# Relative-bias Toeplitz tile: read from one copy of the row and turned round on GpSimd, in place of a 128-fold copy in DRAM

## The chip, the cores and the metric

The kernel runs on one core of one Trainium2 chip. The metric is the device time of one execution in microseconds; before the change it is 1153.88 us, the median of three runs (1153.59 to 1154.02).

## The reference

One decoder layer over 256 tokens of width 2048, all in float32. After a first RMS norm one input projection gives the queries, keys and values of two groups of eight heads (head size 128) and eight forget logits. The first group ("fox") attends causally, with a bias that is a difference of cumulated log forget gates. The second group ("dilated") attends in three patterns of dilation 1, 4 and 16, mixed by their softmax denominators; its bias depends only on the head and on the distance of query and key. Each group's output is normed, both are projected and added to the residual, and a squared-ReLU MLP (2048 to 8192 to 2048) and a final RMS norm follow.

```
logits = einsum('bdhnqe,bdhnke->bdhnqk', qb, kc) * scale
bias   = rel_bias[rel_bucket(clip(rel, 0, span) * dilation)]     # by distance only
logits = logits + bias[None, None, :, None]
```

## The kernel before

**Main stream.** Every weight matrix is read in chunks of 512 columns, and a chunk in steps of 256 rows (two 128-row tiles, `j` = 0 and 1). For each step ScalarE rounds the raw weights to `whi` (L168) and VectorE writes the remainder `wlo` = raw - whi (L169); TensorE then multiplies three terms (L299 to L301, or L313 where the result is wanted turned). For the input projection a step is 12 matmuls. Steps are counted in slots, two to a step; at slot `2*i + j` the side work that was registered with `at(slot, ...)` is emitted right behind the products of that half step. All engines run their own instructions in the order in which they are emitted.

**Supply.** Before the products of step `i`, the splits up to step `i + LEAD` are emitted (`LEAD` = 3), and with the split of step `k` the DMA for step `k + LEAD + 2`, on the SyncE queue; a DMA carries two steps (1 MB) into one of four buffers `raw`. `whi` and `wlo` have four buffers each.

**Around the change.** The first three chunks are q, v and k of four fox heads. The forget logits come with the v chunk, whose last slot is 31. Four slots later `rel_tiles` is emitted: TensorE multiplies the table `relx` with the constant `pick` into a row of 384 biases for each of eight heads (L414), VectorE copies it to SBUF (L416, 8 partitions), and two DMAs on the GpSimd queue follow. L418 writes the row 128 times to DRAM (`rel_d`, 8 x 128 x 384); L419 reads it back with a pitch of 383 per partition, so that partition p gets the row moved by p: that is `relT` (128 x 8 x 256). L419 needs what L418 wrote.

**What is behind it on GpSimd.** `decay_of` (L465) makes the forget-gate operand `gate_h` of a head from `gate_t`; it has two buffers, is emitted three slots before that head's scores, and the first matmul of the scores reads it (L482). The first four heads' scores are at slots 53, 57, 61 and 65, their `values` eleven slots later; each `values` but the first adds a square on GpSimd (L538). The next four fox heads have their scores from slot 101. `relT` is first read by the scores of the third group of heads (L495), whose k chunk is the ninth. Much later `relT` takes the final gains (`load_gf`, L592).

**Buffers.** `big_lo` (`yT_lo`) has 16 head slots; the last eight (`yT_lo[:, NH:, :]`) are first written by `values` of the dilated heads.

Of the kernel before, what the change touches and what calls it, by code (L numbers as in the profile page):

```python
# [11 lines left out]
F32 = mybir.dt.float32  # L12
# [7 lines left out]
P = 128  # L20
D_MODEL = 2048
SEQ = 256
TB = SEQ // P
HD = 128
NH = 8
# [10 lines left out]
RW = 3 * P  # L36
# [6 lines left out]
def _constants():  # L43
    i = np.arange(P)
    upto = (i[:, None] <= i[None, :]).astype(np.float32)
    after = (i[:, None] > i[None, :]).astype(np.float32)
    tri = np.where(i[None, :] <= i[:, None], 0.0, NEG).astype(np.float32)
    head = (i[:, None] % 32 == np.arange(NH)[None, :]).astype(np.float32)
    pack = np.concatenate([after, -upto, tri, np.zeros((P, P), np.float32), tri, head], axis=1)

    dist = 255 - np.arange(RW)
    d = np.maximum(dist, 0)
    exact = N_BUCKETS // 2
    df = np.maximum(d.astype(np.float32), np.float32(1.0))
    large = exact + (
        np.log(df / np.float32(exact)) / np.float32(math.log(REL_MAX / exact)) * np.float32(N_BUCKETS - exact)
    ).astype(np.int32)
    bucket = np.where(d < exact, d, np.minimum(large, N_BUCKETS - 1))
    count = np.zeros(RW, np.int64)
    for window, dil in PATTERNS:  # L60
        count += (dist >= 0) & (dist % dil == 0) & (dist <= window)
    pick = np.zeros((N_BUCKETS + 1, RW), np.float32)
    pick[bucket, np.arange(RW)] = 1.0
    pick[N_BUCKETS] = np.where(count > 0, np.log(np.maximum(count, 1)), NEG)
    return np.ascontiguousarray(pack), pick
# [3 lines left out]
def kernel(  # L69
# [18 lines left out]
    nc = tc.nc  # L88
# [9 lines left out]
    dram = ctx.enter_context(tc.tile_pool(name="dram", bufs=1, space=DRAM))  # L98
# [240 lines left out]
    def at(i, f, *a):  # L339
        side.setdefault(i, []).append((f, a))  # L340
# [66 lines left out]

    relT = one.tile([P, NH, SEQ], F32, name="relT")  # L410

    def rel_tiles():
        p = psum.tile([P, 512], F32, name="sc")
        nc.tensor.matmul(p[:NH, :RW], relx, pick_sb, start=True, stop=True)  # L414
        row = two.tile([P, RW], F32, name="neg")[:NH]
        nc.vector.tensor_copy(row, p[:NH, :RW])  # L416
        d = dram.tile([NH, P, RW], F32, name="rel_d")
        nc.gpsimd.dma_start(d, row[:, None, :].to_broadcast([NH, P, RW]))  # L418
        nc.gpsimd.dma_start(  # L419
            relT, bass.AP(tensor=d.tensor, offset=d.offset + P - 1, ap=[[RW - 1, P], [P * RW, NH], [1, SEQ]])  # L420
        )


    qkv = {}
    yT_hi = one.tile([P, 2 * NH, SEQ], F32R, name="big_hi")
    yT_lo = one.tile([P, 2 * NH, SEQ], F32R, name="big_lo")
# [240 lines left out]
    for ci, (what, key, *_rest) in enumerate(chunks[:-1]):  # L667
        e = last_slot[what, key]
        if what == "v":
            at(e, drain_v, key, ci)  # L670
            if key == 0:
                at(e, drain_f)
                at(e + 2, forget_gates)
                at(e + 6, gate_sums)
                at(e + 4, rel_tiles)
        elif what in "qk":
            late = 3 if ci == 0 else 0
            at(e + late, drain_qk, key, what, ci)
            at(e + late + 2, turn_qk, key, what, 0)
            at(e + late + 3, turn_qk, key, what, 1)  # L680
            if what == "k":
                kind = groups[key][4]
                for h in range(4):
                    n = e + 6 + 4 * h
                    if kind == 0:
                        at(n - 3, decay_of, groups[key][3] * 4 + h)
                    at(n, scores, key, h)
                    at(n + 6, turn_probs, key, h)
                    at(n + 11, values, key, h)
                    if h == 3 and key % 2:  # L690
                        at(n + 13, group_norm, kind)
        elif what == "o":
            at(e, drain_o, *key, ci)
            if key[0] == 1:
                at(e + 2, to_features, 4 * key[1], 16)
                at(e + 3, to_features, 4 * key[1] + 2, 16)
                if key[1] == 3:
                    at(e + 4, second_norm)
        elif what == "u":
            at(e, drain_u, key[1], ci)  # L700
        else:
            at(e, drain_d, *key, ci)
            if key == (ROUNDS - 1, 0):
                at(e - 8, load_gf)
# [68 lines left out]
```

## Time and profile before

| what | value |
|---|---|
| median of 3 runs | 1153.88 us |
| profiled execution | 1154.59 us |
| its span on the core | 1152.8 us |
| mean granted TensorE clock | 0.989 |
| TensorE matmul busy | 1126.7 us, 98% |
| VectorE / ScalarE / GpSimd busy | 55% / 45% / 3% |

The profiled execution's time is 1.8 us longer than the span of the trace, which lies between its first and last instruction. The page says for each engine how long it was busy; the chain of work that ended last goes back from the last instruction, at each step to what released it. A granted clock of 1.00 is 2.4 GHz, 0.50 is 1.2 GHz.

### The profile page before, as it was taken

To read this page: it belongs to the slowest core of one execution; us is meant where nothing else is said; L and a number is where in the kernel's file an instruction comes from. 1 tells how busy PE (TensorE), PEld (TensorE's weight loads), DVE (VectorE), ACT (ScalarE), POOL (GpSimd) and SP (SyncE) were. 2 spreads that over 40 slices of the span, in tenths; PEclk is the share of its full clock that TensorE was granted. 3 is DMA by queue.
4 is the path that set the end of the run, shared out by engine and by line. 5 is a ranking of instruction groups with operands and counts; after the bars stand their busy time and mean duration, and the time that the engine had idled before them with its cause. 6 is when DMAs were issued, how large, how long until landed. Compare 5 with 4: busy or idle time off the path is not lost.

```text
span 1152.8 us, 16038 instructions
## 1 busy us (share of the span) xinstructions
PE 1126.7 (98%) x6635; PEld 991.0 (86%) x6635; DVE 638.9 (55%) x795; ACT 522.0 (45%) x675; POOL 29.4 (3%) x56
## 2 busy tenths in 40 slices
PE   9994999999999999999999999999999999999997
PEld 6773888888888889998889998889999889999886
DVE  5652655656647665555454555544555554555564
ACT  5442544544545455444433544333444343444441
POOL 0100000000000100000000000000000000000000
PEclk9997999999999999999999999999999999999999
DMA  9666455454454455655566465566546666555641
GB/s 314 213 159 161 139 181 183 146 182 147 157 192 162 159 173 180 198 199 189 184 197 195 156 217 184 190 201 194 183 159 209 198 201 183 183 183 184 248 153 73
DMA packets 105605, 210.71 MB, mean 183 GB/s; under 512 B 3987, under 2 KB 4836, under 8 KB 105404
## 3 DMA queue, kind: packets, MB, share of 16 engines
q1 hardware_dynamic: 104556, 207.06, 55.0%
q0 software_dynamic: 976, 2.63, 1.5%
q8 instruction: 52, 0.85, 0.3%
q14 instruction: 21, 0.17, 0.0%
HBM read 206.00 MB, written 3.67 MB: 182 GB/s over the span
## 4 chain that ended last, share of the span: by engine, by line
PE 95%; issue 3%; DVE 1%; DMA 0%; POOL 0%; ACT 0%; SPq 0%; DVEq 0%; POOLq 0%; ACTq 0%
PE acc L313 31%; PE acc L299 20%; PE acc L300 20%; PE acc L301 20%; PE sc L485 1%; PE sc L530 1%; PE tr L250 1%; PE tr L455 1%; PE tr L512 0%; DMA grow<-in_norm_g_dram 0%; PE sc L333 0%; PE sc L482 0%; POOL rel_d L418 0%; ACT L380 0%; DVE wlo L169 0%
## 5 line engine op out<-in xcount | busy, mean ns | idle before, releaser
L169 DVE TENSOR_TENSOR wlo<-raw,whi 128x1024 fp32r<-128x1024 f32 (+1 forms) x381 | 463.3, 1222 | 376.8 <-ACT whi L168 374.0
L168 ACT ACTIVATE whi<-raw 128x1024 fp32r<-128x1024 f32 (+1 forms) x381 | 399.9, 1055 | 406.7 <-PE acc L300 242.9
L313 PE MATMUL acc<-aT_hi,whi 128*128 128x256 f32 x1024 | 287.3, 281 | 0.0
L313 PE MATMUL acc<-aT_lo,whi 128*128 128x256 f32 x1024 | 286.1, 279 | 0.0
L313 PE MATMUL acc<-aT_hi,wlo 128*128 128x256 f32 x1024 | 286.1, 279 | 0.0
L299 PE MATMUL acc<-whi,big_hi 128*128 128x512 f32 (+1 forms) x632 | 246.0, 389 | 0.0
L301 PE MATMUL acc<-wlo,big_hi 128*128 128x512 f32 (+1 forms) x632 | 244.7, 387 | 0.0
L300 PE MATMUL acc<-whi,big_lo 128*128 128x512 f32 (+1 forms) x632 | 244.6, 387 | 0.0
L313 PEld LDWEIGHTS acc<-aT_hi,wlo 128*128 128x128 f32 x1024 | 192.9, 188 | 0.0
L313 PEld LDWEIGHTS acc<-aT_hi,whi 128*128 128x128 f32 x1024 | 192.3, 188 | 0.2
L313 PEld LDWEIGHTS acc<-aT_lo,whi 128*128 128x128 f32 x1024 | 191.7, 187 | 0.2
L299 PE MATMUL acc<-whi,aT_hi 128*128 128x512 f32 x384 | 157.9, 411 | 0.0
L300 PE MATMUL acc<-whi,aT_lo 128*128 128x512 f32 x384 | 153.4, 400 | 0.0
L301 PE MATMUL acc<-wlo,aT_hi 128*128 128x512 f32 x384 | 153.0, 398 | 0.0
L301 PEld LDWEIGHTS acc<-wlo,big_hi 128*128 128x128 f32 x632 | 118.7, 188 | 24.5
L300 PEld LDWEIGHTS acc<-whi,big_lo 128*128 128x128 f32 x632 | 118.8, 188 | 23.2
L299 PEld LDWEIGHTS acc<-whi,big_hi 128*128 128x128 f32 x632 | 118.8, 188 | 23.1
L301 PEld LDWEIGHTS acc<-wlo,aT_hi 128*128 128x128 f32 x384 | 73.1, 190 | 17.6
L299 PEld LDWEIGHTS acc<-whi,aT_hi 128*128 128x128 f32 x384 | 73.3, 191 | 15.4 <-issue 0.6
L300 PEld LDWEIGHTS acc<-whi,aT_lo 128*128 128x128 f32 x384 | 73.4, 191 | 14.2 <-DVE aT_lo L240 0.3
L499 ACT ACTIVATE pr<-neg,st 128x128 f32<-128x128 f32 (+1 forms) x32 | 14.3, 448 | 56.2 <-DVE st L495 56.2
L237 DVE TENSOR_TENSOR big_lo<-nat,big_hi 128x512 fp32r<-128x512 f32 x32 | 22.2, 693 | 22.4 <-ACT big_hi L236 22.4
(159 smaller groups left out, 532.9 us busy)
## 6 DMA issues: line engine op xcount, KB each, us to landing
raw<-in_w_mlp_in_dram SPq DMA_DIRECT2D x64, 1024.0 KB, 5.3
raw<-in_w_mlp_out_dram SPq DMA_DIRECT2D x64, 1024.0 KB, 5.3
raw<-in_w_in_dram SPq DMA_DIRECT2D x42, 1024.0 KB, 5.2
raw<-in_w_out_dram SPq DMA_DIRECT2D x16, 1024.0 KB, 5.1
raw<-in_w_in_dram SPq DMA_DIRECT2D x4, 1040.0 KB, 5.3
raw<-in_w_in_dram SPq DMA_DIRECT2D x3, 512.0 KB, 7.5
xs<-in_x_dram SPq DMA_DIRECT2D x3, 512.0 KB, 9.0
rel_d<-neg POOLq DMA_DIRECT2D x1, 1536.0 KB, 36.6
```

The lines of the kernel that those rows point to most:

```text
L168: nc.scalar.activation(hi, t, AF.Copy)
L169: nc.vector.tensor_tensor(lo, t, hi.bitcast(F32), op=ALU.subtract)
L237: nc.vector.tensor_tensor(lo, src, hi.bitcast(F32), op=ALU.subtract)
L250: nc.tensor.transpose(p[:, j * SEQ + t * P:j * SEQ + (t + 1) * P], xs[:, t, c:c + P], ident)
L299: nc.tensor.matmul(acc, xh, hi[:, j, cols], start=go, stop=False)
L300: nc.tensor.matmul(acc, xl, hi[:, j, cols], start=False, stop=False)
L301: nc.tensor.matmul(acc, xh, lo[:, j, cols], start=False, stop=end)
L313: nc.tensor.matmul(acc, w[:, j, b * P:(b + 1) * P], a[:, kt, :], start=kt == 0 and b % 2 == 0 and n == 0, stop=kt == kts - 1 and n == 2, s ...
L455: nc.tensor.transpose(p[:, j * SEQ + t * P:j * SEQ + (t + 1) * P], ts[t][:, h * P:(h + 1) * P], ident)
L485: nc.tensor.matmul(s[:, c0:c1], q[:, h, t * P:(t + 1) * P], k[:, h, :c1 - c0], start=n == 0 and kind == 1, stop=n == 2,)
L499: nc.scalar.activation(pr[:, c0:c1], neg[:, c0:c1], AF.Exp, bias=st[:, 0, t:t + 1], scale=-1.0, accum_out=st[:, 1, t:t + 1],)
L530: nc.tensor.matmul(y[:, o0:SEQ], v[:, t, h * P:(h + 1) * P], p[:, c0:c1], start=t == 0 and n == 0, stop=t == 1 and n == 2,)
```

## The change

The constant `pick` is built with distances rising instead of falling (`np.arange(RW) - 127`), so the row of biases runs the other way. The row is written to DRAM once (8 x 384). A second DMA reads it with a pitch of 1 per partition, 8 x 256 elements into the unused half of `big_lo`; the keys there run from last to first. A copy on GpSimd with a step of -1 writes `relT` in the right order. The three parts are emitted at slots 35, 36 and 86 (`e` is 31); the second waits for the first, the third for the second.

```
-    dist = 255 - np.arange(RW)
+    dist = np.arange(RW) - 127
...
     relT = one.tile([P, NH, SEQ], F32, name="relT")
-
-    def rel_tiles():
+    rel_d = dram.tile([NH, RW], F32, name="rel_d")
+
+    def rel_row():
         p = psum.tile([P, 512], F32, name="sc")
         nc.tensor.matmul(p[:NH, :RW], relx, pick_sb, start=True, stop=True)
         row = two.tile([P, RW], F32, name="neg")[:NH]
         nc.vector.tensor_copy(row, p[:NH, :RW])
-        d = dram.tile([NH, P, RW], F32, name="rel_d")
-        nc.gpsimd.dma_start(d, row[:, None, :].to_broadcast([NH, P, RW]))
+        nc.gpsimd.dma_start(rel_d, row)
+
+    def rel_back():
         nc.gpsimd.dma_start(
-            relT, bass.AP(tensor=d.tensor, offset=d.offset + P - 1, ap=[[RW - 1, P], [P * RW, NH], [1, SEQ]])
+            yT_lo[:, NH:, :].bitcast(F32), bass.AP(tensor=rel_d.tensor, offset=rel_d.offset, ap=[[1, P], [RW, NH], [1, SEQ]])
         )
+
+    def rel_turn():
+        back = yT_lo[:, NH:, :].bitcast(F32)
+        nc.gpsimd.tensor_copy(relT, bass.AP(tensor=back.tensor, offset=back.offset + SEQ - 1,
+                                            ap=[back.ap[0], back.ap[1], [-1, SEQ]]))
...
-                at(e + 4, rel_tiles)
+                at(e + 4, rel_row)
+                at(e + 5, rel_back)
+                at(e + 55, rel_turn)
```

## Rows read from the trace of the kernel before

**Rows 1.** The page: TensorE's busy time, and its granted clock in 40 slices.
```profile
PE 1126.7 (98%) x6635; PEld 991.0 (86%) x6635; DVE 638.9 (55%) x795; ACT 522.0 (45%) x675; POOL 29.4 (3%) x56
...
PEclk9997999999999999999999999999999999999999
```

**Rows 2.** Chain that ended last, in time: start us, length us, what.
```profile
72.22 1.32 POOL rel_d L418
73.54 35.55 issue
109.13 0.90 POOL relT L419
110.07 0.50 POOL gate_h L465
```

**Rows 3.** Waits of PE: us in total, times, longest us.
```profile
PE sc L482 <- POOL gate_h L465: 15.0, 1, 15.0
```

**Rows 4.** Timeline of PE: start us, us, line, operation, out<-in.
```profile
91.68 0.39 PE L301 MATMUL acc<-wlo,aT_hi 128*128 128x512 f32 x1
...
95.18 0.40 PE L301 MATMUL acc<-wlo,aT_hi 128*128 128x512 f32 x1
110.62 0.47 PE L482 MATMUL sc<-gate_h,gate_s 128*128 128x128 f32 x1 [15.04 <-POOL gate_h L465]
...
112.49 0.63 PE L299 MATMUL acc<-whi,aT_hi 128*128 128x512 f32 x1
...
117.17 0.39 PE L301 MATMUL acc<-wlo,aT_hi 128*128 128x512 f32 x1
...
120.20 0.22 PE L482 MATMUL sc<-gate_h,gate_s 128*128 128x128 f32 x1
...
121.11 0.39 PE L299 MATMUL acc<-whi,aT_hi 128*128 128x512 f32 x1
```

**Rows 5.** Windows: from:to, length, PE's granted clock, DMA share, GB/s.
```profile
95.00:100.00 5.00, 1.00 0.49 64
100.00:105.00 5.00, 0.51 0.51 68
```

**Rows 6.** DMA issues: out<-in, queue, times, KB each, median us to landing.
```profile
rel_d<-neg POOLq DMA_DIRECT2D x1, 1536.0 KB, 36.6
relT<-rel_d POOLq DMA_DIRECT2D x1, 1024.0 KB, 8.8
relT<-in_final_norm_g_dram SPq DMA_DIRECT2D x1, 1024.0 KB, 7.4
out_dram<-xs SPq DMA_DIRECT2D x4, 256.0 KB, 2.4
...
relx<-in_rel_bias_dram SPq DMA_DIRECT2D x1, 1.0 KB, 7.8
```

**Rows 7.** Timeline of POOL.
```profile
49.11 0.20 POOL L158 CAST wf<-raw 128x16 fp32r<-128x16 f32 x1 [3.22 <-PE sc L333]
...
155.15 0.73 POOL L538 TENSOR_TENSOR sq<-sq,sqt 128x256 f32<-128x256 f32 x1 [5.53 <-ACT sqt L536]
155.87 0.93 POOL L465 TENSOR_SCALAR gate_h<-gate_t,pk 128x256 fp32r<-128x256 f32 x2
...
376.00 1.59 POOL L538 TENSOR_TENSOR sq<-sq,sqt 128x256 f32<-128x256 f32 x1 [5.75 <-ACT sqt L536]
```

**Rows 8.** Timeline of DVE.
```profile
90.20 0.69 DVE L237 TENSOR_TENSOR k_lo<-tr,k_hi 128x512 fp32r<-128x512 f32 x1 [1.68 <-ACT k_hi L236]
...
375.76 1.22 DVE L169 TENSOR_TENSOR wlo<-raw,whi 128x1024 fp32r<-128x1024 f32 x1
```

**Rows 9.** Windows of L169 on DVE, then of L301 on PE and PEld: busy (instructions).
```profile
0.00:95.41 95.41, 36.11 (x31) 0.98 0.72 221
...
0.00:95.41 95.41, 43.00 (x108) 20.60 (x108) 0.98 0.72 221
```

**Rows 10.** Tile raw from 40 to 140 us: landing times of its loads.
```profile
DMA to landing us min/median/max: 4.9/5.6/32.2
```

## Prediction

> **What bounds the kernel now.** I read the page first: TensorE's matmuls are busy 98% of the span, and the granted clock is low in one slice only after the start, the fourth, 86 to 115 us [rows 1]. So TensorE is the bound, and a change elsewhere counts only through a hole in its stream. The view of waits, for TensorE alone, has one long row: 15.0 us, once, for `gate_h` of L465 [rows 3]. The chain of waits says where that comes from [rows 2]: L418 issues the 128-fold copy at 72.22 us; the next 35.55 us no engine does anything that the chain can name; then L419, and only behind it `gate_h` at 110.07. GpSimd works in order, L419 waits for what L418 wrote, and L465, which needs nothing of either, stands behind L419. That the wait is the copy's is in the DMA view: the 1536 KB of `rel_d` take 36.6 us from issue to landing [rows 6].
>
> **What the wait costs.** The last product before the hole starts at 95.18 us; the row 15 matmuls earlier starts at 91.68, so the pitch is 0.233 us and the scores were due at 95.41. They start at 110.62: 15.21 us lost [rows 4]. A second loss follows. The clock is 1.00 from 95 to 100 us and 0.51 from 100 to 105, that is, it falls from 2.4 to 1.2 GHz inside the idle time [rows 5], and TensorE starts again slow. From 110.62 to 117.17 it runs 19 matmuls, the eight of the scores and eleven products, in 6.55 us. At the full clock the same eight scores take 0.91 us (120.20 to 121.11) and eleven products 11 x 0.233 = 2.56: 3.47 us. Lost: 3.08 us [rows 4]. Together 18.29 us.
>
> **The change part by part.** *The constant and the matmul:* the same sizes; zero by construction.
>
> *L418, now 12 KB instead of 1536 KB, and the wait of `rel_back` for it.* No row shows a 12 KB write on this queue. From below: 2.4 us, the stores of 256 KB to DRAM. From above: the old 36.6 us, if the time were fixed and not that of the bytes; against that speaks the other DMA of the same queue, which lands 1024 KB in 8.8 us, so there is no fixed cost above 8.8 [rows 6]. A load of 1 KB between weight loads took 7.8 us. I take 5 us, nearer to the small transfers; ends 2.4 and 8.8. Issue as before 1.32 us, so `rel_back` goes out at 72.22 + 1.32 + 5 = 78.5 us (75.9 to 82.3), takes 0.90 us on GpSimd as L419 does, and the two waiting `gate_h` another 0.93 [rows 2, 7]: done at 80.4 us (77.8 to 84.2), where the scores want them at 95.41. Eleven microseconds are to spare at the late end. The hole is gone if the 12 KB land in under 95.41 - 73.54 - 1.83 = 20 us.
>
> *`rel_back`:* the same 1 MB in the same pieces of 1 KB as L419, which landed in 8.8 us; what is new is that all partitions read the same 12 KB. The load of the final gains also reads one 8 KB row for all 128 partitions, and lands 1024 KB in 7.4 us [rows 6]. I take 8.8; bounds 7.4 and 36.6 (if it fared like `rel_d`). Nothing on GpSimd waits for it before `rel_turn`. In exchange the 36.6 us write leaves the DMA engines: beside it one weight load took 32.2 us where the median is 5.6 [rows 10]. TensorE showed no wait for that, because it was standing still; so no gain is booked, but the weights are better off, not worse.
>
> *`rel_turn`, 128 x 2048 on GpSimd.* It is emitted at slot 86, behind the third square sum of the first heads (slot 76), whose row is at 155.15 us and would move to 136.9. GpSimd is idle there until the `gate_h` of the next heads, which have run at 155.87 until now and are wanted for slot 101. That is 15 slots of half a step (6 x 0.233 = 1.4 us) behind slot 86, 21 us at least. Its length is on no row. Two sizes of one-input work are: 0.20 us for 16 elements per partition and 0.47 for 256 (half of 0.93), so 0.27 / 240 = 1.1 ns an element and 0.20 + 2032 x 0.0011 = 2.5 us. From above by a plausible row, eight times the two-input sum of 0.73: 5.8 us; from above by any row, 16 elements in 0.20 us, 12.5 ns each: 25.6 us [rows 7]. I take 3 us, near the one-input rows; a step of -1 has no row and is why the upper end is kept.
>
> It can cost something only through VectorE. A square sum that starts at 376.00, while `wlo` runs from 375.76 to 376.98, lasts until 377.59, 0.61 after that end, against 0.73 alone [rows 7, 8]: GpSimd did nothing until `wlo` was over. No row shows the opposite, a `wlo` kept waiting by GpSimd. If it waits as long as the copy runs, `wlo` is up to 3 us late. Cover: at 95.41 TensorE had done 108 matmuls of L301, four to a step, so 27 steps; VectorE had begun 31 `wlo`, of which the first two are halves of one step, so 30 steps [rows 9]. The newest `wlo` is thus wanted two whole steps later, 2 x 12 x 0.233 = 5.6 us, some 6 with its own rest. A turn of up to 6 us costs nothing, one of T us costs about T - 6; with 3 us zero, by the bounds 0 to 19.6 us.
>
> The Trainium skill, "SBUF — State Buffer", section "Who interferes with whom", says that a VectorE instruction with two SBUF inputs and a GpSimd instruction that reads SBUF exclude each other, for the whole of whichever starts first. The trace agrees where VectorE was first, 1.59 us against 0.73; no run here shows the other order. By that rule a `wlo` would wait out the whole copy; by the row alone it need not wait; with 6 us of cover the sum is the same, and the rule is the rival below when the copy is long. The skill's "GPSIMD Engine Reference", section 3.1, gives 1.8 cycles an element at best for one-input loops, which would make 3.1 us at 1.2 GHz, an estimate from that page.
>
> *What is late next,* at the scores of slot 53: `k_lo` of those heads is written at 90.89 [rows 8], before 95.41, and three split steps are in hand [rows 9]. The other sets of scores wait for nothing, by the same view in which the 15.0 is the one long row [rows 3].
>
> **Sum.** 1154.59 (profiled) - 15.21 - 3.08 + 0 = 1136.3 us. The profiled execution is 0.71 above the median of the runs, so the median goes from 1153.88 to 1135.6.
>
> **Rivals.** (a) *The turn blocks VectorE for longer than its cover.* With T between 6 and 15 us TensorE waits 0 to 9 us around 140 us, without the clock loss while the hole is under the 4 us or so that it took to fall [rows 5], with 3.1 us beyond: 1135.6 to 1147.7; I give 1139 at T = 9.4. For it: the excluding seen at 376 us. Against: the one-input rows at 1.1 ns.
> (b) *The read of one hot row is slow and starves the weights.* If `rel_back` takes 36.6 us and holds a weight load for 32.2 [rows 10], that load, issued five steps (14.0 us) ahead of its split and 6 more ahead of its use, is 12 us late; with 3.1 of clock 1150.7. Against: the gains' load at 7.4 us.
> (c) *The wait is not one of bytes* and `rel_back` still holds GpSimd for 36 us: the hole stays, 1154. Against: 8.8 us on the same queue.
> (d) *Slower:* `rel_turn` costs what the tiny casts cost, 12.5 ns an element, 25.6 us. Then `wlo` stops for that time at about 138 us, TensorE for 25.6 - 6 = 19.6 and 3.1 us of slow clock on top: 22.7 - 18.3 = 4.4 slower, 1158.3. It decides from T = 6 + 18.3 - 3.1 = 21.2 us on, 10.3 ns an element. For it: only that a backward step is on no row.
>
> **Chances.** Forecast 0.82 with its own spread of 1134 to 1137.5; (a) 0.09; (b) 0.03; (c) 0.03; (d) 0.03. The range 1133.5 to 1141 takes in the forecast and most of (a). About 0.2% (2.3 us) is what a measurement of this kernel can tell from no change. Faster is the forecast, (a) and (b), 0.94; same is (c), 0.03; slower is (d), 0.03.
>
> **What would show it.** Right: no wait of TensorE for `gate_h`; the two `gate_h` at about 80 us; granted clock 1.00 from 95 to 120 us; products following the first scores at a pitch of 0.233; a `rel_turn` of 2.5 to 6 us at about 137 us with at most one `wlo` pushed back and no hole in TensorE behind it; no weight load over 10 us between 72 and 90. Wrong: `rel_back` issued after 93 us, a wait of TensorE for `wlo` around 140 us, or a `rel_turn` beyond 6 us.

## The result and the profile after

The changed kernel takes 1137.01 us (median of 4, 1136.27 to 1137.23) against 1153.74 us before: a ratio of 0.9855 with a 95% interval of 0.9838 to 0.9872, 16.7 us. The forecast was 1135.6 us, the range 1133.5 to 1141. The profiled execution took 1136.86 us, 17.73 less than that of before; its span is 1135.1 us.

GpSimd after the change (timeline: start us, length us, line, operation, out<-in):

```profile
72.81 0.76 POOL L419 DMA_DIRECT2D rel_d<-neg  x1 [22.62 <-DVE neg L418]
77.00 0.96 POOL L422 DMA_DIRECT2D big_lo<-rel_d  x1 [3.44 <-DVE wlo L169]
78.00 0.94 POOL L473 TENSOR_SCALAR gate_h<-gate_t,pk 128x256 fp32r<-128x256 f32 x2
...
137.47 0.73 POOL L546 TENSOR_TENSOR sq<-sq,sqt 128x256 f32<-128x256 f32 x1 [5.53 <-ACT sqt L544]
138.15 1.90 POOL L428 COPY relT<-big_lo 128x2048 f32<-128x2048 f32 x1
140.03 1.90 POOL L473 TENSOR_SCALAR gate_h<-gate_t,pk 128x256 fp32r<-128x256 f32 x2
```

The read-back goes out 4.2 us after the write, where it took 36.9 before [rows 2], and the two `gate_h` are ready at 78.9 us, 17 us before they are wanted. (The view names `wlo` as what released the read-back; in a second profile of the change it names the 12 KB write itself, 3.66 us of idle time, and the write landed there in 4.1.) The issues, KB and us to landing:

```profile
big_lo<-rel_d POOLq DMA_DIRECT2D x1, 1024.0 KB, 7.3
...
rel_d<-neg POOLq DMA_DIRECT2D x1, 12.0 KB, 3.9
```

TensorE, its waits (us in total, times, longest) and its stream at the first scores:

```profile
PE sc L220 <- DVE relx L199: 1.2, 1, 1.2
PE tr L250 <- DVE aT_lo L240: 0.8, 1, 0.8
PE tr L227 <- DMA grow<-in_norm_g_dram: 0.5, 1, 0.5
```

```profile
95.76 0.40 PE L301 MATMUL acc<-wlo,aT_hi 128*128 128x512 f32 x1
95.99 0.22 PE L490 MATMUL sc<-gate_h,gate_s 128*128 128x128 f32 x1
...
96.91 0.39 PE L299 MATMUL acc<-whi,aT_hi 128*128 128x512 f32 x1
...
102.51 0.22 PE L490 MATMUL sc<-gate_h,gate_s 128*128 128x128 f32 x1
```

The 15.0 us row for `gate_h` [rows 3] is gone; what is left are three waits of the start. The scores follow the products at the pitch of 0.23 us and take 0.92 us, and the next set follows 6.52 us behind, where it took 9.58 [rows 4]. The granted clock of the stretch (from:to, length, clock, DMA share, GB/s) is 1.00, against 0.51 at 100 to 105 before [rows 5]:

```profile
95.00:100.00 5.00, 1.00 0.64 209
100.00:105.00 5.00, 1.00 0.36 88
```

The weight loads between 40 and 140 us land in 8.4 us at the worst, where one took 32.2 [rows 10]:

```profile
DMA to landing us min/median/max: 5.0/5.2/8.4
```

### The profile page after: what moved, and what is told of

It reads as the page before. It is cut to its first block, busy times and chain, and to the rows that moved or that the text cites. A ratio compares the mean times of both kernels' runs of the same rounds, so it can differ in the third digit from the quotient of the medians.

```text
span 1135.1 us, 16038 instructions
## 1 busy us (share of the span) xinstructions
PE 1124.0 (99%) x6635; PEld 988.8 (87%) x6635; DVE 639.7 (56%) x795; ACT 521.9 (46%) x675; POOL 31.7 (3%) x57
## 4 chain that ended last, share of the span: by engine, by line
PE 98%; DMA 1%; DVE 0%; SPq 0%; ACT 0%; POOL 0%; issue 0%; DVEq 0%
PE acc L313 32%; PE acc L299 21%; PE acc L301 21%; PE acc L300 21%; PE sc L493 1%; PE sc L538 1%; PE tr L463 1%; DMA raw<-in_w_in_dram 1%; PE tr L250 1%; PE tr L520 0%; PE sc L333 0%; PE sc L490 0%; DVE wlo L169 0%; ACT whi L168 0%; DVE xs L646 0%; SPq L185 0%
## 5 line engine op out<-in xcount | busy, mean ns | idle before, releaser
L169 DVE TENSOR_TENSOR wlo<-raw,whi 128x1024 fp32r<-128x1024 f32 (+1 forms) x381 | 464.1, 1224 | 374.4 <-ACT whi L168 371.6
L301 PE MATMUL acc<-wlo,big_hi 128*128 128x512 f32 (+1 forms) x632 | 244.7, 387 | 0.0
L301 PE MATMUL acc<-wlo,aT_hi 128*128 128x512 f32 x384 | 152.3, 397 | 0.0
L301 PEld LDWEIGHTS acc<-wlo,big_hi 128*128 128x128 f32 x632 | 118.7, 188 | 24.4
L301 PEld LDWEIGHTS acc<-wlo,aT_hi 128*128 128x128 f32 x384 | 72.5, 189 | 17.4
```

The lines of the kernel that those rows point to most:

```text
L169: nc.vector.tensor_tensor(lo, t, hi.bitcast(F32), op=ALU.subtract)
L301: nc.tensor.matmul(acc, xh, lo[:, j, cols], start=False, stop=end)
```

## The experiments

**Same kernel again.** To see whether the 16.7 us are steady.

> The changed kernel, unchanged, in five rounds: whether its gain is the 18.3 us of the sum (1135.4 with before at 1153.7) or the 16.7 of the first runs. Theory: the stretch from 60 us on gives 18.3 in every profile, and what differs is the start, the first 15 us, in which the scatter of the first loads moves the whole stream by some 0.6 us to either side; the ratio should come to lie between 0.9840 and 0.9855. Rival: the changed kernel loses a steady 1 us somewhere (start, or VectorE behind the turn), and the ratio stays at 0.9855 with a narrow interval.

Measured 1136.74 us (1136.50 to 1136.92) against 1153.21: ratio 0.9852 (0.9837 to 0.9867), inside the band of the theory and of the rival alike: the gain is 16.5 us here and 16.7 above, not 18.3. What decides between them is the next pair.

**The kernel before, profiled twice more.** No edit.

> The kernel before, profiled again: how much the hole and the start differ from one execution to the next. Theory for the 1.2 to 1.8 us by which the measured gain falls short of 18.3: the profiled execution on which the sum rests was a long one (1154.59 against 1153.2 to 1153.9 in the runs), because its 128-fold copy landed late; another profile shows the scores 0.5 to 1.5 us closer to the row of biases (L414 to L482: 42.58 us in the first) and a span nearer to 1151.5. Rival (the changed kernel loses about a microsecond at its start): L414 again at 68.0 us, against 68.6 and 68.7 in both profiles of the change.

> The same once more, for a second sample of the start (L414 at 68.0 to 68.8 us) and of the hole (L414 to L482, 41 to 43 us).

Measured 1155.89 and 1153.30 us, one run each. Rows of the first and of the second of these: the row of biases, the first scores, the next scores, and in the second (the third profile in all) the last product at the slow clock and the first at the full one.

```profile
69.94 0.81 PE L414 MATMUL sc<-pr,relx 33*8 33x384 f32 x2
...
111.85 0.47 PE L482 MATMUL sc<-gate_h,gate_s 128*128 128x128 f32 x1 [14.38 <-POOL gate_h L465]
...
121.49 0.22 PE L482 MATMUL sc<-gate_h,gate_s 128*128 128x128 f32 x1
```

```profile
68.68 0.81 PE L414 MATMUL sc<-pr,relx 33*8 33x384 f32 x2
...
110.70 0.47 PE L482 MATMUL sc<-gate_h,gate_s 128*128 128x128 f32 x1 [14.49 <-POOL gate_h L465]
...
113.43 0.63 PE L301 MATMUL acc<-wlo,aT_hi 128*128 128x512 f32 x1
...
114.23 0.39 PE L300 MATMUL acc<-whi,aT_lo 128*128 128x512 f32 x1
...
118.90 0.22 PE L482 MATMUL sc<-gate_h,gate_s 128*128 128x128 f32 x1
```

Cut at these three rows into four pieces, the spans of all five profiles read (us):

| profile | start to L414/L416 | to first scores | to next scores | rest of span |
|---|---|---|---|---|
| before, first | 68.04 | 42.58 | 9.58 | 1032.6 |
| before, second | 69.94 | 41.91 | 9.64 | 1032.6 |
| before, third | 68.68 | 42.02 | 8.20 | 1032.6 |
| after | 68.62 | 27.37 | 6.52 | 1032.6 |
| after, again | 68.69 | 27.36 | 6.52 | 1032.5 |

The changed kernel loses nothing behind the row of biases: its middle pieces, without a wait and at the full clock, are the same in both profiles. Against them the kernel before has a hole (the time in which TensorE stands still) of 14.54 to 15.21 us and loses 1.68 to 3.12 us in the slow stretch behind it: in the third profile TensorE was back at 2.4 GHz 3.5 us after the first score, in the other two after about 6.6. The start takes 68.0 to 69.9 us before, and 68.0 to 68.9 in the eight profiles of the change and of its variants below with one copy.

So the theory that every profile gives 18.3 us from the row of biases on falls: the three give 18.27, 17.66 and 16.33. That the first had the longest hole holds, by 0.56 and 0.67 us; the span came near 1151.5 in the third profile alone, for the second started late, at 69.94, which stays unexplained. The rival, a start that the change makes later, falls: the third profile starts at 68.68 too.

**Only the order on GpSimd.** The 128-fold copy stays.

```
         nc.gpsimd.dma_start(d, row[:, None, :].to_broadcast([NH, P, RW]))
+        rel_ds.append(d)
+
+    def rel_read():
+        d = rel_ds[0]
         nc.gpsimd.dma_start(
...
                 at(e + 4, rel_tiles)
+                at(e + 55, rel_read)
```

> The kernel before with its 128-fold copy, and only the read-back (the DMA that waits for the copy) moved from slot 35 to slot 86, behind the gate_h of the first heads. Theory (the gain is the hole in TensorE alone, made by what stands behind the waiting DMA on GpSimd): no wait for gate_h, ratio to before as for the change, about 0.985, 1136 to 1137.5 us. Rival (the 1.5 MB write itself is what the change takes away: beside it a weight load took 32.2 us, and TensorE would wait for weights once it no longer waits for gate_h): a wait of TensorE for wlo of about 12 us between 95 and 115 us, 1146 to 1151 us.

Measured 1143.53 us, ratio 0.9911 (0.9896 to 0.9926): between the two, in the band of neither. The scores start on time, 27.37 us behind the row of biases. But TensorE runs dry some ten microseconds later. Its first product after this hole, the landing times of the weight loads from 40 to 140 us, and the granted clock, DMA share and GB/s meanwhile:

```profile
110.80 0.80 PE L299 MATMUL acc<-whi,aT_hi 128*128 128x512 f32 x1 [4.03 <-ACT whi L168]
```

```profile
DMA to landing us min/median/max: 4.9/6.2/31.6
```

```profile
95.00:100.00 5.00, 1.00 0.52 68
100.00:105.00 5.00, 1.00 0.48 64
```

The last row before the hole is at 106.28 (three transposes, 0.33 us), so the hole is 4.2 us. Behind it seven products take 3.50 us, 1.63 at full pitch, so the slow clock costs 1.9 us; together these are the 6.1 us by which its span (1141.2) is longer than that of the change. So both are true: of the 16.5 us between the medians of before and of the change in this set of runs the order alone gives 9.7, and the smaller write the other 6.8, because the copy also held up weight loads. The load that TensorE waited for was out at 77.99 us and took 31.6. Before the change that second wait lay hidden behind the first: the same load, out at 77.3 us, took 32.2 [rows 10] and landed at 109.5, just ahead of the scores at 110.62.

**Fewer copies.** The changed kernel, with the row written 80 or 100 times and the last copy read.

```
-    rel_d = dram.tile([NH, RW], F32, name="rel_d")
+    COPIES = 80
+    rel_d = dram.tile([NH, COPIES, RW], F32, name="rel_d")
...
-        nc.gpsimd.dma_start(rel_d, row)
+        nc.gpsimd.dma_start(rel_d, row[:, None, :].to_broadcast([NH, COPIES, RW]))
...
-            offset=rel_d.offset, ap=[[1, P], [RW, NH], [1, SEQ]]
+            offset=rel_d.offset + (COPIES - 1) * RW, ap=[[1, P], [COPIES * RW, NH], [1, SEQ]]
```

> The kernel after, but the row is written 80 times before it is read back (the last copy is read). By a straight line between the landing times of 1 copy (3.9 us) and 128 copies (36.6 us): 24.2 us, gate_h ready at 98.5 us where the scores are due at 96.0. Theory: a hole of about 2.5 us, and no second loss, since the clock fell only some 4.5 us into the old hole: about 1139.5 us, scores at 0.91 us. Rival (the slow clock is a price of any hole): 3.1 us more, 1142.6. Rival (time is not linear in the copies): no hole, or all of it.

> As the last, with 100 copies. By the same line 29.4 us, gate_h at 103.7 us, a hole of 7.7 us, which is longer than the clock stayed up in the old one: 7.7 + 3.1 = 10.8 us over the changed kernel, about 1147.8 us. If the second loss shrinks with the hole, 1146 us; if there is none, 1144.7.

Measured 1138.22 us with 80 and 1146.24 us with 100. The landing of the write and TensorE's wait, first with 80, then with 100 copies, and the granted clock with 100:

```profile
rel_d<-neg POOLq DMA_DIRECT2D x1, 960.0 KB, 22.8
```

```profile
PE sc L491 <- POOL gate_h L474: 1.3, 1, 1.3
```

```profile
rel_d<-neg POOLq DMA_DIRECT2D x1, 1200.0 KB, 28.3
```

```profile
PE sc L491 <- POOL gate_h L474: 6.8, 1, 6.8
```

```profile
95.00:100.00 5.00, 0.97 0.50 74
100.00:105.00 5.00, 0.50 0.91 338
```

The landing times 3.9, 22.8, 28.3 and 36.6 us for 1, 80, 100 and 128 copies lie near a line of 0.26 us a copy, 1.4 and 1.1 us under it in the middle. With 80 the first scores come 28.81 us after the row of biases (27.37 without a hole) and the next 6.61 us later (6.52): 1.4 us of hole, no slow clock, and the kernel is 1.5 us longer than the change. The rival of a slow clock behind any hole falls. With 100 they come after 34.31 and 8.41: 6.9 of hole and 1.9 of slow clock, nearest to the middle one of the three expectations; since that loss was 1.68 to 3.12 behind the full hole, one profile does not show that it shrinks with the hole. A short hole costs itself; the slow clock came with holes of 4.2 us and more, not with 1.4.

**No turn.** The additions of the dilated scores read the reversed tile directly.

```
-            add = mcat[:, c0:c1] if kind == 0 else relT[:, hd, SEQ - (c1 - c0):]
+            add = mcat[:, c0:c1] if kind == 0 else turned_rel(hd, c1 - c0)
...
+    def turned_rel(hd, n):
+        back = relT[:, hd, :n]
+        return bass.AP(tensor=back.tensor, offset=back.offset + n - 1, ap=[back.ap[0], [-1, n]])
...
-                at(e + 55, rel_turn)
```

> The changed kernel without the turn: the read-back lands in relT with the keys from last to first, and the additions of the dilated scores (L503) read it with a step of -1. Theory (the turn is wholly covered): same time as the change, 1136.7 +- 0.5; the 16 additions that read relT backwards keep their 291 and 421 ns. Rival (the turn costs part of the 1.2 to 1.8 us that are missing, by holding VectorE): about 1 us faster, 1135.5. Rival (a backward operand is slow on VectorE): additions twice as long, and still the same time, as VectorE is busy 56%.

Measured 1136.54 us, ratio 0.9854 (0.9837 to 0.9870): the same. The additions are as long backwards as forwards; their durations in ns (min/median/max) are 291/356/420 in the change, and here:

```profile
L502 DVE CUSTOM_DVE_ANT_0 neg<-sc,relT x16: 291/356/421, 250.3 to 346.0; 128x128 f32<-128x128 f32 x8, 128x256 f32<-128x256 f32 x8
```

The turn costs nothing, and leaving it out gains nothing.

**Turn first.** `at(e + 6, rel_turn)` in place of `at(e + 55, rel_turn)`.

> The changed kernel with the turn emitted at slot 37 in place of 86, ahead of the gate_h of the first heads, so that GpSimd waits for the read-back before it. Theory (only the time at which gate_h is ready counts, against 96.0 us): read-back lands at 77.0 + 7.3 = 84.3 us, turn to 86.2 or a little later, gate_h at 87.1 to 88.5 us, no wait in TensorE, same time as the change (1136.7). Rival (a second DMA wait on GpSimd opens the hole again): gate_h after 96 us, and as many microseconds longer.

```profile
83.94 1.90 POOL L428 COPY relT<-big_lo 128x2048 f32<-128x2048 f32 x1 [6.03 <-DMA big_lo<-rel_d]
85.82 1.91 POOL L473 TENSOR_SCALAR gate_h<-gate_t,pk 128x256 fp32r<-128x256 f32 x2
```

Measured 1136.76 us, no wait. GpSimd may stand still 6 us for the read-back in front of `gate_h`, which is ready at 87.7 all the same, 8 us early. It is the time of `gate_h` that counts and not the wait as such.

**Forward copy.** The step of the copy is 1.

> The changed kernel with the copy on GpSimd at a step of +1, which leaves the keys of the dilated bias in the wrong order: the price of the backward step. Theory: none, 1.90 us as with -1. Rival: shorter by half or more.

```profile
137.75 1.90 POOL L428 COPY relT<-big_lo 128x2048 f32<-128x2048 f32 x1
```

One run, 1136.44 us. The copy takes 1.90 us either way: the backward step is free. With the 0.20 us of the 16-element cast [rows 7] taken off, (1.90 - 0.20) / 2032 makes 0.84 ns an element, an estimate.

**Ten turns, and two long instructions.** How deep is VectorE's cover? First the turn in a loop of ten, then one wasted addition in front of it:

```
+        wide = yT_lo[:, NH:, :].bitcast(BF16)
+        nc.gpsimd.tensor_tensor(relT.bitcast(BF16), wide, wide, op=ALU.add)
```

and last the same with operands `ap=[w.ap[0], [1, 16], [16, 256]]`.

> The changed kernel with the turn done ten times in a row. One turn is 1.90 us in the profile of the change, and a wlo that met it took 1.93 us in place of 1.23. Theory (GpSimd and VectorE take turns, each waits at most for the other's running instruction): the ten end after some 25 to 30 us, each wlo in the stretch takes 1.3 to 3.1 us, VectorE stays within its six microseconds of cover, no hole, same time as the change (1136.7). Rival (ten instructions of GpSimd keep VectorE out for all their 19 us): wlo stops, a hole of 13 us and a slow clock of 3, about 1153.

> The changed kernel with one long wasted instruction on GpSimd ahead of the turn: an addition of 128 x 4096 bf16, the words of the read-back taken as bf16, written to relT and then overwritten by the turn. By eight times the 0.73 us of a two-input sum of 256 elements, doubled: up to 11.7 us, by the slope of smaller rows some 9. Theory (the exclusion of a two-input VectorE instruction holds for the whole instruction of GpSimd, and the cover is about 6 us): one wlo of about 8 to 11 us, TensorE waits 2 to 6 us around 148 us, 1139 to 1145. Rival (VectorE gets in between, or has more cover): no wlo longer than some 3 us, no hole, 1136.7.

> As the long addition, with the two operands read at a step of 32 bytes (the same 4096 bf16 words in another order), to make the one instruction longer than the 7.01 us that the last one took; nothing of this case shows how much longer, I guess 10 to 12 us. There a wlo was held until 1.1 us after the instruction's end, 5.8 us late, and TensorE did not wait. Theory (exclusion for the whole instruction, cover about 6 us): with a length L the wlo ends L - 1.2 us late, and TensorE waits for L - 1.2 - 6, that is 3 to 5 us at 10 to 12, time 1139.5 to 1144.5. Rival (the cover is deeper than I count): no hole and 1136.7. If L stays at 7, the run tells nothing new.

Ten turns: 1136.44 us. GpSimd's row, and the longest `wlo` in it:

```profile
137.55 27.50 POOL L429 COPY relT<-big_lo 128x2048 f32<-128x2048 f32 x10
```

```profile
160.99 2.31 DVE L169 TENSOR_TENSOR wlo<-raw,whi 128x1024 fp32r<-128x1024 f32 x1 [0.53 <-ACT whi L168]
```

The engines alternate: the turns stretch from 19 to 27.5 us, nine of the ten `wlo` in that time from 1.23 to between 1.94 and 2.31, and TensorE waits for none. The rival of ten in a row falls.

One long addition: 7.01 us, shorter than I had put it, and 1136.62 us. One `wlo` takes 7.06 us; it ends 1.08 us after GpSimd's instruction, 5.8 us late, and TensorE does not wait:

```profile
137.99 7.01 POOL L429 TENSOR_TENSOR relT<-big_lo 128x4096 bf16<-128x4096 bf16 x1
```

```profile
139.02 7.06 DVE L169 TENSOR_TENSOR wlo<-raw,whi 128x1024 fp32r<-128x1024 f32 x1 [0.99 <-ACT whi L168]
```

The longer one: 8.75 us, and 1138.31 us, ratio 0.9866 (0.9850 to 0.9883). The `wlo` is 7.6 us late, and now TensorE waits:

```profile
138.48 8.75 POOL L430 TENSOR_TENSOR relT<-big_lo 128x4096 bf16<-128x4096 bf16 x1
```

```profile
139.52 8.80 DVE L169 TENSOR_TENSOR wlo<-raw,whi 128x1024 fp32r<-128x1024 f32 x1 [0.99 <-ACT whi L168]
```

```profile
PE acc L301 <- DVE wlo L169: 0.9, 1, 0.9
```

7.6 late and 0.9 of wait: the cover (how late a `wlo` may be before TensorE waits) is 6.7 us, where the count of steps gave some 6 and so 1.6 of wait. By medians the kernel is 1.3 to 1.6 us longer than the change, of which the wait is 0.9. My guesses of the two lengths (9 to 12 us) were too high; the rule for what they cost held with that cover.

## Why the prediction was right, and where its size was off

- *What bounds, and the hole.* Right. TensorE waited for `gate_h` because L465 stood behind L419; with the wait gone the scores run on at full pitch and clock.
- *The size.* The sum said 18.29 us, the runs say 16.7 and 16.5. Between the two profiles it is exact: the pieces from the row of biases on differ by 15.21 + 3.06 = 18.27 us, less a start that was 0.58 us later after, which is the 17.7 of the spans. What was off is the last step of the sum, where 18.29 us from one execution were taken off the median of the runs. That execution was known to be 0.71 us longer than the median, and the sum put none of this into the hole; its hole was in fact the longest of three, by 0.56 and 0.67 us. The clock's term of 3.08 was measured as 3.06, 3.12 and 1.68: in the third profile the two terms make 16.3 us. Which size is the common one stays open, for no execution at the median of before was profiled. In the 28 runs of the kernel before that stand beside the experiments the mean granted clock is 0.989 in two (the first two profiles: 0.989), 0.990 in seventeen, and 0.991 or 0.992 in nine (the third: 0.991).
- *The write of 12 KB.* Taken at 5 us, measured 3.9 and 4.1.
- *`rel_back`, one hot row.* Taken at 8.8 us, measured 7.3, as the gains' load, 7.4 [rows 6]. Rival (b) falls for this change. A slow transfer that starves the weights is real, as the order experiment shows for the write, but I priced it too high: 12 us and 3 of clock against 4.2 and 1.9. The weight load there was out at 77.99 us and TensorE ran dry at 106.6, so a load is 28.6 us ahead of its use in that stretch, not the 20 that I counted.
- *"No gain is booked" for the DMA engines.* Right in the sum, incomplete as a reading. The write costs 6 us by itself once the hole is closed in another way; I had the row for it [rows 10] and used it for a rival only.
- *`rel_turn`.* Taken at 3 us, measured 1.90, below the 2.5 to 6 that I gave as a sign of being right; rivals (a) and (d) fall with that. The excluding of the two engines, of which the rows showed one order, goes both ways: in the change a `wlo` that starts at 139.20 lasts 1.93 us and ends 1.08 us behind the turn.

```profile
139.20 1.93 DVE L169 TENSOR_TENSOR wlo<-raw,whi 128x1024 fp32r<-128x1024 f32 x1 [0.99 <-ACT whi L168]
```

The Trainium skill, "SBUF — State Buffer", section "Who interferes with whom", says just that, an exclusive hold for the whole of the instruction that was first, and the 7.06 and 8.80 us of the long additions agree with it. The Trainium skill's "GPSIMD Engine Reference", section 3.1, was read too narrowly: its 1.8 cycles an element are for an unrolled loop, 3.1 us as an estimate at 1.2 GHz, and for the shortest loop bodies the same section gives 1.03 cycles, 1.8 us as an estimate. The 1.90 us measured lies near the second.

- *Rival (c)* falls with the landing of 3.9 us; over 1, 80, 100 and 128 copies the landing time grew nearly on a straight line with what is written.

## What to carry to other kernels

Where an engine issues a DMA that waits for another DMA, look at what is queued behind it on that engine: here two half-microsecond instructions that needed neither held TensorE for 15 us. Before you book the whole hole, look for a second lateness that hides in its shadow, and ask what each way of closing it would uncover. And the hole and the slow stretch behind it differed between executions, by 0.67 and 1.44 us here: take such a loss from several profiles before you set it against a median.

## What the runs showed of the hardware that I had not expected

- From 95 to 105 us, while the 128-fold write and the weight loads beside it were all that moved, the mean DMA share was 0.50 at 64 to 68 GB/s [rows 5]. The write's 1536 KB took 36.6 us, where a read of 1024 KB on the same queue took 7.3; and a weight load issued beside it took nearly as long as the write, 32.2 us [rows 10]. What in the write makes it slow (its eight source partitions, the one source read 128 times, or the writing to DRAM) was not tried.
- After a hole of about 15 us TensorE ran on at 1.2 GHz for about 6.6 us in two profiles and for 3.5 in a third, with the same work.
- A read of 12 KB of DRAM by all 128 partitions (1 MB moved) landed in 7.3 and 7.7 us in the two profiles of the change, as the read of the copies laid out apart did in the order experiment, 7.3. Right behind a long write both are slower: 9.4 and 11.5 us from one copy with 100 and 80 copies, 8.8 us apart before the change [rows 6]. And a backward step costs nothing on GpSimd (1.90 us) or VectorE (356 ns).
